# Six more small slots ahead of the stage pools, and a later place in the queue for the first seven-product pair's loads

## The chip, the cores and the metric

The kernel runs on one core of one Trainium2 chip. The metric is the device time of one execution in microseconds (us), the median of several runs. A profile records one further execution with the start and duration of every instruction and every DMA packet; it shows five engines: TensorE (PE for its matmuls, PEld for the loads of their stationary operands), VectorE (DVE), ScalarE (ACT), GpSimd (POOL) and SyncE (SP, which here only issues DMAs).

## What is computed

A decoder layer over 256 tokens of width 2048, batch 1, all in float32: a half-step SwiGLU block, a mixer (dilated attention beside gated linear attention, with one input and one output projection), cross-attention into 256 memory tokens, and a second half-step SwiGLU block.

```python
def swiglu(h, w_gate, w_up, w_down):
    return (jax.nn.silu(h @ w_gate) * (h @ w_up)) @ w_down

for l in range(DEPTH):                       # DEPTH = 1
    x = x + 0.5 * swiglu(rms_norm(x, ffn1_norm[l]), ffn1_w_gate[l], ffn1_w_up[l], ffn1_w_down[l])
    x = x + hybrid_mixer(rms_norm(x, mix_norm[l]), ...)
    x = x + cross_attention(rms_norm(x, xattn_norm[l]), rms_norm(mem, mem_norm[l]), ...)
    x = x + 0.5 * swiglu(rms_norm(x, ffn2_norm[l]), ffn2_w_gate[l], ffn2_w_up[l], ffn2_w_down[l])
return x
```

The gate and up weights of each SwiGLU block are 2048 x 5632, the down weights 5632 x 2048; together they are most of the 392 MB that the kernel reads.

## The kernel before

**Precision.** Every float32 operand of the large products is split in two parts, a high part rounded to the matmul's fp32r type and the low rest (`hi`, `lo`; `wh`, `wl` for weights). A product is three matmuls: high by high, high by low, low by high. In each, the moving operand is a 128 x 512 piece of a weight (`wh` or `wl`) and the stationary operand a 128 x 128 block of activations. ACT makes `wh` by a copy that rounds, DVE makes `wl` by a subtraction, both in halves of 128 x 1024 of a weight tile `raw` of 1 MiB that a DMA brought.

**Stages.** A SwiGLU block runs over eleven chunks `f` of 512 hidden columns. For `f == 0` `proj` (lines 165 to 181) makes gate and up in turn from four weight tiles each, loaded by `wgroup` (line 142). For every other `f`, `seven` (lines 249 to 286) makes gate and up together as a 2 x 2 block product with seven block products in place of eight (`product`, lines 223 to 227) and four plain ones (`plain`); its weight tiles are called `b11`, `b21`, `b12` and `b22` in the code, and DVE adds tiles to `b11` in place (`add`, line 205). After each of three segments of chunks, `proj` with the down weights runs over the chunks' hidden values `hT`. "The first pair" below is the gate and up of chunk `f == 1` in the first block, the first call of `seven`.

**What sets the order.** The kernel is written as one program, and a planner orders it for each engine by priority: an instruction's place in the program, less an offset that `tc.high_priority(n)` gives. Weight loads and splits of `wgroup` and the splits of `parts` have offset `WPRI = 200`; the loads of `seven`, through `load` (line 187), have `LPRI = 400`; the loads of `x` have `XPRI = 170` less 12 a chunk. All loads but one kind go through SP's queue in that order; the exception is the gate tile that POOL's queue adds to `b12` in memory (line 209). A load also needs a free buffer. The 1 MiB tiles have four buffers (`RB = 4`) that `wgroup` and `load` share; three tiles of each `seven` (`b11`, `b12`, `b22`, marked `True`) have three buffers of their own in a stage pool (`RX = 3`).

**Where tiles lie.** Pools are laid out along a partition in the order in which they are opened: `con` (constants, the residual `x`, and the transposed input `xTh`/`xTl`), `wp` (`raw`, `wh`, `wl`), `sp` (small work tiles of 2 KiB), `st` (statistics of 4 to 16 bytes, ten slots), and then the pools of a stage, opened by `enter` (lines 69 to 76): `u`, 26 or 32 slots of 2 KiB, and in the two SwiGLU blocks `r`, the three 8 KiB buffers above. The layout of the compiled kernel before, in bytes within a partition:

| tiles | pool | first address | past a multiple of 512 |
|---|---|---|---|
| `xTh`, `xTl` (stationary) | `con` | 33,824 | 32 |
| `raw`; `wh`; `wl` (moving) | `wp` | 67,104; 99,872; 116,256 | 32 |
| ten slots of 32 bytes | `st` | 149,024 | 32 |
| `hTh`, `hTl`, `Fh`, `Fl`, `mTh`, `mTl`, `memh`, `meml`, `oh`, `ol` (stationary) and others | `u` | 149,344 | 352 |
| `b11`, `b12`, `b22` | `r` | 202,592 | 352 |

All slots of these pools are a multiple of 512 bytes long, and each 128 x 128 block takes 512 bytes of a partition, so every block of a pool starts at the same distance past a multiple of 512. `hT` are the hidden values (stationary operand of the down projection), `F` three of the five differences of activation blocks that `seven` uses (the other two are written over blocks of `xTh`/`xTl` in `con`, line 388), `mT` the mixer's heads (output projection), `mem` the memory tokens, `o` the cross-attention's heads.

Of the kernel before, what the change touches and what calls it, by code (L numbers as in the profile page):

```python
# [27 lines left out]
WPRI = 200  # L28
LPRI = 400
# [25 lines left out]
def layer_kernel(ctx: ExitStack, tc: tile.TileContext, A: dict, out: bass.AP):  # L55
# [3 lines left out]
    con = ctx.enter_context(tc.tile_pool(name="con", bufs=1))  # L59
    wp = ctx.enter_context(tc.tile_pool(name="wp", bufs=3))  # L60
    sp = ctx.enter_context(tc.tile_pool(name="sp", bufs=SB))
    st = ctx.enter_context(tc.tile_pool(name="st", bufs=10))
    pa = ctx.enter_context(tc.tile_pool(name="pa", bufs=4, space=PSUM))
    pm = ctx.enter_context(tc.tile_pool(name="pm", bufs=4, space=PSUM))

# [12 lines left out]
    def U(shape, dt, name):  # L78
        return stage["u"].tile(shape, dt, tag="u", name=name)

    def raw_tile(long=False):

        if long and "r" in stage:
            return stage["r"].tile([P, 4, 512], F32, tag="rawx", name="raw")
        return wp.tile([P, 4, 512], F32, tag="raw", name="raw", bufs=RB)
# [3 lines left out]
    def W2(shape, name, dt=F32):  # L89
        return sp.tile(shape, dt, tag="w", name=name)  # L90
# [4 lines left out]
    def PM(shape, name):  # L95
        return pm.tile(shape, F32, tag="ps", name=name)
# [4 lines left out]
    def later(n, fn):  # L101
        pend.append([n, fn])
# [81 lines left out]


    def load(src, long=False):
        with tc.high_priority(LPRI):
            raw = raw_tile(long)
            SY.dma_start(raw, src)
        return raw  # L190
# [12 lines left out]
    def add(dst, src):  # L203
        with tc.high_priority(WPRI):
            V.tensor_add(dst, dst, src)  # L205

    def add_hbm(dst, src):
        with tc.high_priority(WPRI):
            G.dma_start(dst, src, accum_op=ALU.add)

    def urgent(op, *args, **kw):

        with tc.high_priority(FPRI):
            op(*args, **kw)  # L214
# [8 lines left out]
    def product(bank, form, raw, start):  # L223

        for h, half in enumerate(parts(raw)):
            mms(bank, form, half, start and h == 0, h == 1)
            tick()

    def plain(banks, forms, raw, start, order):
        for h, half in enumerate(parts(raw)):  # L230
            for t in order:
                mms(banks[t], forms[t], half, start[t] and h == 0, h == 1)
            tick()
# [4 lines left out]
    def difference(x, name, home=None):  # L238

        a, b = PAIRS[name]  # L240
        with tc.high_priority(WPRI):
            d = W2([P, 4, P], "d")
            V.tensor_sub(d, x[a], x[b])
            hi, lo = home or (U([P, 4, P], F32R, "Fh"), U([P, 4, P], F32R, "Fl"))
            SC.copy(hi, d)
            V.tensor_sub(lo, d, hi.bitcast(F32))
        return hi, lo

    def seven(ld, F, A12, A21, pair, others, rest):

        k1, k2 = pair
        Y, Z, X, R = [pa.tile([P, 512], F32, tag="acc", name="acc") for _ in range(4)]
        b11 = load(ld(0, k1), True)
        b21 = load(ld(0, k2))
        add(b11, b21)
        product(Y, A21, b11, True)
        s21 = W2([P, 512], "s21")
        urgent(SC.copy, s21, Y)  # L260
        b12 = load(ld(1, k1), True)
        product(Z, F["22-21"], b21, True)
        add(b11, b12)
        product(Y, F["12-21"], b11, False)
        s22 = W2([P, 512], "s22")
        urgent(SC.copy, s22, Y)
        b22 = load(ld(1, k2), True)
        product(X, F["22-12"], b22, True)
        add(b11, b22)
        product(R, A12, b11, True)  # L270
        urgent(V.tensor_sub, s22, R, s22)
        product(Y, F["21-11"], b12, False)
        add_hbm(b12, ld(0, k1))
        s12 = W2([P, 512], "s12")
        urgent(SC.copy, s12, Y)
        for k in others:
            plain((R, X), (rest(0, k), rest(1, k)), load(ld(1, k)), (False, False), (1, 0))
        urgent(V.tensor_sub, s12, R, s12)
        urgent(V.tensor_add, s22, X, s22)
        for k in others[:-1]:  # L280
            plain((Y, Z), (rest(0, k), rest(1, k)), load(ld(0, k)), (False, False), (1, 0))
        product(Y, F["11-12"], b12, False)
        k = others[-1]
        plain((Y, Z), (rest(0, k), rest(1, k)), load(ld(0, k)), (False, False), (0, 1))
        urgent(V.tensor_add, s21, Z, s21)
        return Y, s21, s12, s22

    def split_from_psum(hi, lo, ps):
        SC.copy(hi, ps)
        V.tensor_sub(lo, ps, hi.bitcast(F32))  # L290
# [70 lines left out]
    def ffn(pre, r, after, fine=None, last=False):  # L361
        wg, wu, wd = (A[f"{pre}_w_{n}"] for n in ("gate", "up", "down"))
        hT = {}
        F, xf = {}, {}

        def turn(f, hs):
            for t in range(TT):
                hi = U([P, 4, P], F32R, "hTh")
                lo = U([P, 4, P], F32R, "hTl")
                tp = PM([P, 4, P], "tp")  # L370
                for j in range(4):
                    PE.transpose(tp[:, j], hs[t][:, j * P:(j + 1) * P], ident)  # L372
                split_from_psum(hi, lo, tp)
                hT[f, t] = (hi, lo)

        def x_block(t, c):
            return tuple(p[:, :, t * P:(t + 1) * P] for p in xT[c])

        def x_differences(names):

            if not xf:
                for c in range(2):
                    for t in range(TT):
                        xf[t, c] = U([P, 4, P], F32, "xf")
                        hi, lo = (p.bitcast(F32) for p in x_block(t, c))
                        with tc.high_priority(WPRI):
                            V.tensor_add(xf[t, c], hi, lo)
            homes = {"21-11": x_block(1, 1), "11-12": x_block(0, 0)}
            for name in names:
                F[name] = difference(xf, name, homes.get(name))  # L390

        def lhs_h(k, t):
            return tuple(p[:, k % 4] for p in hT[k // 4, t])

        for seg in SEGS:
            for f in seg:
                if f == 0:
                    acc = proj(wg, f, lhs_x, range(4), fine)
                    if callable(r):
                        r = r()  # L400
                    later(DIFF, lambda: x_differences(("22-21", "12-21", "22-12")))
                    later(DIFF + 4, lambda: x_differences(("21-11", "11-12")))
                else:
                    y, s21, s12, s22 = seven(lambda col, k: (wg, wu)[col][f, k], F, x_block(0, 1), x_block(1, 0),
                                             (0, 1), (2, 3), x_block)
                    acc = [y, s21]
                sg = []
                for t in range(TT):
                    s = acc[t] if f and t else W2([P, 512], "sg")
                    urgent(SC.activation, s, acc[t], AF.Silu, scale=r[:, t:t + 1])  # L410
                    sg.append(s)
                acc = [s12, s22] if f else proj(wu, f, lhs_x, range(4))
                hs = []
                for t in range(TT):
                    h = acc[t] if f else W2([P, 512], "h")
                    urgent(V.scalar_tensor_tensor, h, acc[t], r[:, t:t + 1], sg[t], op0=ALU.mult, op1=ALU.mult)
                    hs.append(h)
                later(TURN, lambda f=f, hs=hs: turn(f, hs))
            final = seg is SEGS[-1]
            for c in range(NC):  # L420
                acc = proj(wd, c, lhs_h, seg, last=last and final and c == NC - 1)
                for t in range(TT):
                    V.scalar_tensor_tensor(xs[c][:, t], acc[t], 0.5, xs[c][:, t], op0=ALU.mult, op1=ALU.add)
                if final:
                    after(c)
# [57 lines left out]

    ss2 = new_ss("ss2")
    ffn("ffn1", load_x, lambda c: norm_chunk(c, xs[c], 16, ss2), fine=first)
    r2 = rstd_of(ss2, "r2")
    enter(u=UM)
# [479 lines left out]
    def store(c):  # L967
        for t in range(TT):
            SC.dma_start(out[0, t * P:(t + 1) * P, c * 512:(c + 1) * 512], xs[c][:, t])

    ffn("ffn2", r4, store, last=True)
    stage["stack"].close()
    assert not pend
# [83 lines left out]
```

## Time and profile before

| | |
|---|---|
| median of 3 runs | 1977.75 us (1976.2 to 1978.92) |
| the profiled execution's own time | 1978.33 us |
| its span, first to last instruction | 1976.2 us |
| granted TensorE clock, mean | 0.997 of full speed |
| DVE busy | 1377.3 us (70%) |
| ACT busy | 1062.0 us (54%) |
| POOL busy | 78.9 us (4%) |
| moved by DMA | 395.24 MB, 200 GB/s on average |

The views used below: the page with the busy time of each engine and the chain of work that ended last; the timeline, one row for an instruction or a run of equal ones, with its start and duration in us, engine, line, operation, tiles and, in brackets, the idle time before it and what ended that; the stretches, with the busy time of each engine and in brackets its instructions, then the granted clock, the DMA engines' share and their rate; and the groups of instructions by line with their count, busy time and mean duration. A matmul's recorded duration is longer than the distance from its start to the next one's start, since matmuls overlap; that distance is called the pitch here.

### The profile page before, as it was taken

Reading aid. Unit: us, or ns where it says so; the run is one execution under the profiler, and the core shown is the slowest. Engines: PE = TensorE matmul, PEld = TensorE weight load, DVE = VectorE, ACT = ScalarE, POOL = GpSimd, SP = SyncE. Lnnn points to the kernel's source line nnn. Section 1 sums busy time; section 2 is a strip of 40 time slices with the busy share of each in tenths; the row PEclk is TensorE's granted clock in tenths of the full one; section 3 lists DMA queues with packets and bytes.
Section 4 is the critical chain, followed back from the end, with each engine's and each line's share of the span. In section 5 each row is a group of like instructions: output and inputs, shape, how many; then the busy total and the mean of one; then the engine's idle time right before and its main releaser. Section 6 shows DMA issues by size and latency. Waiting matters only on the chain.

```text
span 1976.2 us, 22472 instructions
## 1 busy us (share of the span) xinstructions
PE 1951.9 (99%) x8760; PEld 1582.7 (80%) x8760; DVE 1377.3 (70%) x1423; ACT 1062.0 (54%) x1305; POOL 78.9 (4%) x81
## 2 busy tenths in 40 slices
PE   8999999999999999999999999999999999999999
PEld 6788887888878888778888779888887888887787
DVE  5888568885588664546785465888747888568863
ACT  5566346654356546544575365656634655436642
POOL 1000000000000000002220000000000000000000
PEclk9999999999999999999999999999999999999999
DMA  9566546775556554435465454666654766546563
GB/s 362 171 229 239 180 160 224 224 247 199 192 192 213 174 181 171 171 134 202 174 230 194 181 181 150 234 212 214 234 190 162 223 234 234 193 169 213 192 211 108
DMA packets 60566, 395.24 MB, mean 200 GB/s; under 512 B 6795, under 2 KB 7947, under 8 KB 14252
## 3 DMA queue, kind: packets, MB, share of 16 engines
q1 hardware_dynamic: 56428, 370.74, 51.4%
q0 software_dynamic: 2880, 20.97, 5.8%
q10 hardware_dynamic: 1152, 2.10, 0.3%
q8 instruction: 68, 1.11, 0.2%
q14 instruction: 38, 0.31, 0.0%
HBM read 391.69 MB, written 2.10 MB: 199 GB/s over the span
## 4 chain that ended last, share of the span: by engine, by line
PE 81%; DVE 12%; issue 3%; DMA 2%; ACT 2%; POOL 0%; SPq 0%; ACTq 0%; POOLq 0%
PE acc L161 17%; PE acc L163 17%; PE acc L162 17%; PE acc L220 9%; PE acc L221 9%; PE acc L219 9%; DVE wl L200 7%; DVE raw L205 2%; DMA raw<-in_ffn_w_gate_dram 2%; DVE s L214 1%; ACT wh L199 1%; DVE hTl L290 1%; PE tp L330 0%; DVE wl L153 0%; PE tp L372 0%
## 5 line engine op out<-in xcount | busy, mean ns | idle before, releaser
L153 DVE TENSOR_TENSOR wl<-raw,wh 128x1024 fp32r<-128x1024 f32 (+1 forms) x370 | 452.5, 1226 | 377.0 <-ACT wh L152 375.0
L152 ACT CAST wh<-raw 128x1024 fp32r<-128x1024 f32 (+1 forms) x370 | 386.5, 1047 | 466.8 <-PE acc L163 403.6
L199 ACT CAST wh<-raw 128x1024 fp32r<-128x1024 f32 x440 | 456.4, 1053 | 307.2 <-PE acc L221 251.3
L200 DVE TENSOR_TENSOR wl<-raw,wh 128x1024 fp32r<-128x1024 f32 x440 | 522.1, 1220 | 87.9 <-ACT wh L199 84.2
L220 PE MATMUL acc<-wl,xTh 128*128 128x512 f32 x960 | 375.8, 391 | 5.0 <-DVE wl L200 4.1
L219 PE MATMUL acc<-wh,xTh 128*128 128x512 f32 x960 | 375.9, 392 | 0.7
L221 PE MATMUL acc<-wh,xTl 128*128 128x512 f32 x960 | 373.7, 389 | 0.0
L161 PE MATMUL acc<-wh,hTh 128*128 128x512 f32 x704 | 278.3, 395 | 0.0
L163 PE MATMUL acc<-wh,hTl 128*128 128x512 f32 x704 | 277.5, 394 | 0.0
L162 PE MATMUL acc<-wl,hTh 128*128 128x512 f32 x704 | 277.5, 394 | 0.0
L161 PE MATMUL acc<-wh,xTh 128*128 128x512 f32 x544 | 217.0, 399 | 8.4 <-ACT wh L152 6.1
L220 PEld LDWEIGHTS acc<-wl,xTh 128*128 128x128 f32 x960 | 180.2, 188 | 50.0 <-DVE wl L200 13.0
L219 PEld LDWEIGHTS acc<-wh,xTh 128*128 128x128 f32 x960 | 180.2, 188 | 45.8 <-ACT wh L199 8.9
L163 PE MATMUL acc<-wh,xTl 128*128 128x512 f32 x544 | 214.3, 394 | 0.9 <-DVE xTl L314 0.9
L162 PE MATMUL acc<-wl,xTh 128*128 128x512 f32 x544 | 214.6, 394 | 0.3 <-DVE wl L153 0.3
L221 PEld LDWEIGHTS acc<-wh,xTl 128*128 128x128 f32 x960 | 180.2, 188 | 37.0
L205 DVE TENSOR_TENSOR raw<-raw 128x2048 f32<-128x2048 f32 x60 | 137.3, 2289 | 55.3 <-DMA raw<-in_ffn_w_gate_dram 54.6
L163 PEld LDWEIGHTS acc<-wh,hTl 128*128 128x128 f32 x704 | 131.7, 187 | 32.6
L162 PEld LDWEIGHTS acc<-wl,hTh 128*128 128x128 f32 x704 | 131.8, 187 | 32.2
L161 PEld LDWEIGHTS acc<-wh,hTh 128*128 128x128 f32 x704 | 131.7, 187 | 32.0
L161 PEld LDWEIGHTS acc<-wh,xTh 128*128 128x128 f32 x544 | 103.5, 190 | 30.9 <-ACT wh L152 6.1
L163 PEld LDWEIGHTS acc<-wh,xTl 128*128 128x128 f32 x544 | 103.4, 190 | 23.0 <-DVE xTl L314 1.3
(279 smaller groups left out, 1793.4 us busy)
## 6 DMA issues: line engine op xcount, KB each, us to landing
raw<-in_ffn_w_up_dram SPq DMA_DIRECT2D x88, 1024.0 KB, 4.9
raw<-in_ffn_w_down_dram SPq DMA_DIRECT2D x88, 1024.0 KB, 4.8
raw<-in_ffn_w_gate_dram SPq DMA_DIRECT2D x85, 1024.0 KB, 4.8
raw<-in_w_in_dram SPq DMA_DIRECT2D x48, 1024.0 KB, 4.8
raw<-in_ffn_w_gate_dram POOLq DMA_DIRECT2D x20, 1024.0 KB, 8.9
raw<-in_w_out_dram SPq DMA_DIRECT2D x16, 1024.0 KB, 4.8
raw<-in_xattn_w_k_dram SPq DMA_DIRECT2D x4, 1024.0 KB, 4.8
raw<-in_xattn_w_q_dram SPq DMA_DIRECT2D x4, 1024.0 KB, 4.8
```

Source lines behind the costliest of these rows:

```text
L152: SC.copy(wh[:, d], src)
L153: V.tensor_sub(wl[:, d], src, wh[:, d].bitcast(F32))
L161: PE.matmul(acc[t], lh, wh, start=first and i == 0, stop=False)
L162: PE.matmul(acc[t], lh, wl, start=False, stop=False)
L163: PE.matmul(acc[t], ll, wh, start=False, stop=last and i == len(half) - 1)
L199: SC.copy(wh, src)
L200: V.tensor_sub(wl, src, wh.bitcast(F32))
L205: V.tensor_add(dst, dst, src)
L214: op(*args, **kw)
L219: PE.matmul(bank, hi[:, k], wh, start=start and i == 0, stop=False, skip_group_check=True)
L220: PE.matmul(bank, hi[:, k], wl, start=False, stop=False, skip_group_check=True)
L221: PE.matmul(bank, lo[:, k], wh, start=False, stop=stop and i == len(half) - 1, skip_group_check=True)
```

## The change

The pool `st` gets 16 slots in place of 10, and the offset with which `load` places its loads becomes a variable. It is `WPRI` for chunk 1 of the first block and `LPRI` for all others, as before.

```diff
-    st = ctx.enter_context(tc.tile_pool(name="st", bufs=10))
+    st = ctx.enter_context(tc.tile_pool(name="st", bufs=16))
...
     def load(src, long=False):
-        with tc.high_priority(LPRI):
+        with tc.high_priority(ahead[0]):
             raw = raw_tile(long)
             SY.dma_start(raw, src)
         return raw
...
+    ahead = [LPRI]
...
                 else:
+                    ahead[0] = WPRI if f == 1 and pre == "ffn1" else LPRI
                     y, s21, s12, s22 = seven(lambda col, k: (wg, wu)[col][f, k], F, x_block(0, 1), x_block(1, 0),
                                              (0, 1), (2, 3), x_block)
```

With slots of 32 bytes, six more of them put the first address of `u` at 149,536 and that of `r` 192 bytes higher too, 32 bytes past a multiple of 512. No instruction is added or taken away, and the pools opened before `st` stay where they are.

## The prediction

> **What bounds the kernel now.** I read the page first: how busy each engine is, and which engine the chain of work that ended last runs through.
>
> ```profile
> span 1976.2 us, 22472 instructions
> PE 1951.9 (99%) x8760; PEld 1582.7 (80%) x8760; DVE 1377.3 (70%) x1423; ACT 1062.0 (54%) x1305; POOL 78.9 (4%) x81
> PE 81%; DVE 12%; issue 3%; DMA 2%; ACT 2%; POOL 0%; SPq 0%; ACTq 0%; POOLq 0%
> ```
>
> PE is busy for all but 24 us, and four fifths of the chain are its own. So time goes only if matmuls follow each other faster, or if one of the few places goes where PE waits. The change offers one of each.
>
> To see how fast matmuls follow each other I took two long stretches without a wait from the timeline, one with stationary operands in pool `u` (`hT`), one with stationary operands in `con` (`xT`), and asked the view of the stretches for their counts.
>
> ```profile
> 202.74 0.40 PE L162 MATMUL acc<-wl,hTh 128*128 128x512 f32 x1
> 286.04 0.39 PE L162 MATMUL acc<-wl,hTh 128*128 128x512 f32 x1
> 1258.47 0.39 PE L163 MATMUL acc<-wh,xTl 128*128 128x512 f32 x1
> 1299.07 0.39 PE L220 MATMUL acc<-wl,xTh 128*128 128x512 f32 x1
> ```
>
> ```profile
> 202.75:286.20 83.45, 83.45 (x359) 66.91 (x358) 45.17 (x40) 31.61 (x32) 0.00 (x0) 1.00 0.51 177
> 1258.50:1299.20 40.70, 40.70 (x181) 33.70 (x180) 33.08 (x38) 23.57 (x28) 0.70 (x1) 1.00 0.56 203
> ```
>
> A matmul's record lasts longer than the pitch, so a count also holds the matmul before the stretch's first row, which is still running. From the row at 202.74 to that at 286.04 there are therefore 359 - 2 = 357 pitches: 83.30 / 357 = 0.2333 us. From 1258.47 to 1299.07 there are 181 - 2 = 179: 40.60 / 179 = 0.2268. The clock is 1.00 in both, PE never waits, shapes and moving operands (`wh`, `wl`) are the same. A matmul whose stationary block lies in `u` costs **6.5 ns more**. By the layout the two kinds differ in the distance past a multiple of 512 (352 against 32) and in the region of the partition (above 149 KB against 34 to 67 KB). The trace cannot part these two, and that is the main uncertainty.
>
> The second place is at the start.
>
> ```profile
> 10.48 0.33 SPq L189 DMA_DIRECT2D raw<-in_ffn_w_gate_dram  x1
> 12.53 1.02 SPq L189 DMA_DIRECT2D raw<-in_ffn_w_up_dram  x2
> 14.48 0.33 SPq L142 DMA_DIRECT2D raw<-in_ffn_w_gate_dram  x1
> 15.14 1.62 SPq L304 DMA_DIRECT2D xr<-in_xT_dram  x2
> ```
>
> ```profile
> 28.42 1.99 ACT L152 CAST wh<-raw 128x1024 fp32r<-128x1024 f32 x2 [7.82 <-DMA raw<-in_ffn_w_gate_dram]
> 29.42 3.02 POOL L312 TENSOR_TENSOR xr<-xr,gain 128x512 f32<-128x512 f32 x2 [10.43 <-DMA xr<-in_xT_dram]
> 28.50 0.39 PE L163 MATMUL acc<-wh,xTl 128*128 128x512 f32 x1
> 31.16 0.50 PE L161 MATMUL acc<-wh,xTh 128*128 128x512 f32 x1 [2.28 <-ACT xTh L313]
> 33.04 0.80 PE L163 MATMUL acc<-wh,xTl 128*128 128x512 f32 x1 [0.95 <-DVE xTl L314]
> 39.17 0.40 PE L162 MATMUL acc<-wl,xTh 128*128 128x512 f32 x1
> ```
>
> ```profile
> 28.50:39.20 10.70, 7.47 (x19) 5.24 (x18) 7.99 (x7) 7.33 (x11) 3.02 (x2) 0.68 1.03 407
> DMA packets 3419, 14.47 MB, mean 414 GB/s; under 512 B 323, under 2 KB 323, under 8 KB 2205
> ```
>
> The last line is the DMA view of 12 to 47 us: the engines are saturated at 414 GB/s. Three 1 MiB loads of the first pair (10.48, 12.53) stand ahead of the fourth gate tile of chunk 0 (14.48) and the last blocks of the input (15.14), which land near 28.4 and 29.4 and are what ACT and POOL wait for. PE stops after 28.50, restarts in pieces, and then runs at a lower granted clock: 0.68 over the stretch.
>
> **The change part by part.** *A, the shift.* It moves no pool but `u` and `r`. The products with a stationary block in `u`, one row of each kind of three equal ones:
>
> ```profile
> L161 PE MATMUL acc<-wh,hTh 128*128 128x512 f32 x704 | 278.3, 395 | 0.0
> L219 PE MATMUL acc<-wh,Fh 128*128 128x512 f32 x240 | 96.8, 403 | 1.2 <-ACT wh L199 1.2
> L161 PE MATMUL acc<-wh,mTh 128*128 128x512 f32 x128 | 51.0, 399 | 0.9 <-DVE x L885 0.9
> L161 PE MATMUL acc<-wh,memh 128*128 128x256 f32 x64 | 18.6, 290 | 0.0
> L161 PE MATMUL acc<-wh,oh 128*128 128x512 f32 x32 | 12.9, 404 | 0.0
> L161 PE MATMUL acc<-wh,memh 128*128 128x512 f32 x32 | 12.8, 401 | 0.0
> ```
>
> - `hT`: 3 x 704 = 2112 by 6.5 ns = 13.7 us. The group has no idle time: PE sets the pace, so it counts in full.
> - `mT`, `oh`, `memh` at 512 columns: 3 x (128 + 32 + 32) = 576 by 6.5 = 3.7 us; `memh` at 256 columns: 192 by half of it, an estimate, 0.6 us.
> - `F`: 720 by 6.5 = 4.7 us at most, and none of it if something else sets the pace there. I asked for the chain of one pair:
>
> ```profile
> 106.58 1.24 DVE wl L200
> 122.28 1.23 DVE wl L200
> 123.55 0.50 PE acc L220
> ```
>
> ```profile
> 113.81 0.48 PE L219 MATMUL acc<-wh,Fh 128*128 128x512 f32 x1
> 123.10 0.39 PE L221 MATMUL acc<-wh,Fl 128*128 128x512 f32 x1
> ```
>
> From 106.58 to 123.51 the chain is on DVE (`wl`, the additions to `b11`, the evacuations) and comes back to PE only at 123.55; all `F` matmuls of the pair run from 113.81 to 123.10, beside it. A quicker `F` matmul only waits longer for `wl`. I take **0 of the 4.7**.
>
> The new pitch in `u` is not shown. Bounds: 0.2333 (nothing gained) and 0.2268 (the row of `con`); a rise is the third rival below. I take 0.2268, as that row has the very offset, 32, that `u` will have. The other instructions on shifted tiles do not care, by the rows of the one subtraction that writes to both places:
>
> ```profile
> L246 DVE TENSOR_TENSOR Fl<-d,Fh x6: 685/686/693, 53.3 to 1281.5; 128x512 fp32r<-128x512 f32 x6
> L246 DVE TENSOR_TENSOR xTl<-d,xTh x4: 683/686/687, 56.2 to 1287.9; 128x512 fp32r<-128x512 f32 x4
> ```
>
> Behind a quicker `hT` stretch nothing is late: in its row above DVE is busy 45.17 and ACT 31.61 of 83.45 us, and DMA takes 0.51. Six more slots of `st` cost no instruction, and the change adds no wait. Sum of A: 13.7 + 3.7 + 0.6 = **18.0 us** (18.0 to 22.7 if it works).
>
> *B, the loads.* All loads of the first pair lose 200 places. Three of them move in SP's queue from ahead of the gate tile at 14.48 to behind everything of chunk 0: that gate tile, two input blocks and four up tiles (and the four loads of `x`); POOL gets its `xr` earlier too. Three tiles are 3.15 MB; at 414 GB/s that is 7.6 us. So the gate tile lands near 28.4 - 7.6 = 20.8 and the input blocks near 21.8; from the last landing to PE's third restart it took 33.04 - 29.42 = 3.6 us, so all is ready at 25.4, **3.1 us before** PE ends at 28.50. The stop goes, and the lower clock that followed it. From 28.50 to 39.17 PE began 17 matmuls after the first (19 in the stretch's row, less the one still running and the first itself); at 0.2268 these take 3.9 us in place of 10.67: **6.8 us** gained.
>
> What can be late next is the first pair itself. Its first work is an addition to `b11`:
>
> ```profile
> 59.18 2.29 DVE L205 TENSOR_TENSOR raw<-raw 128x2048 f32<-128x2048 f32 x1
> ```
>
> It would start 6.8 us earlier, at 52.4. Queued in the new order, up to and with the pair's four tiles: the input 2.1 MB, gate and up 8.4, `x` 2.1, the four 4.2, together 16.8 MB; at 414 GB/s 40.6 us, about 45 us with a slower start (an estimate). That is 7 us of cover; without it each late 1 MiB costs 2.5 us. Bounds of B: 0 (the stop comes back elsewhere) to 6.8.
>
> Sum: 18.0 + 6.8 = 24.8. The profiled execution took 1978.33 us (its span and 2.1 around it), so 1953.5; it lies 0.6 above the median of the runs, so **1952.9 us** for the median.
>
> **A rule against A.** The Trainium skill, "TensorE: Matmul & The Clock Gate", section "Step-by-step: what each phase is for", says that TensorE has two independent read ports and that loading the next stationary operand takes no bandwidth from the running matmul; "SBUF — State Buffer", section "Specifications (TRN2)", gives lines of 16 bytes, of which 352 and 32 both are multiples. By these the offset would change nothing and A would bring 0. This trace does not agree with so simple a picture: equal shapes at an equal clock stand at 0.2333 and 0.2268. What no row excludes is that the region, and not the offset, makes the difference.
>
> **The rivals.**
> 1. *A does nothing*, since the region decides: `u` stays above 149 KB and its pitch at 0.2333. For it: the two kinds differ in both ways. Against, this row of the tile view (minimum, median and maximum duration): `hT` tiles lie in slots all over `u`, and the 704 durations keep within 5 ns, as if the one thing that all slots share decided.
>
> ```profile
> L162 PE MATMUL acc<-wl,hTh x704: 393/394/398, 196.3 to 1971.4; 128*128 128x512 f32 x176
> ```
>
>    Time: 1977.75 - 6.8 = 1971.
> 2. *B is given back* in the first pair. Its later loads now have offset 200, while the second pair's first loads keep 400. A pair is some 250 places long (180 matmuls and some 70 others, by the code), so those rank about 250 - 200 = 50 places behind the first pair's first load, ahead of its plain tiles, and can take one of the four shared buffers. A plain tile then comes late, PE stops as it did after 28.50, and the price is the same 6.8 us. For it: the inversion of ranks. Against: plain tiles are used behind five of the seven products, and three shared buffers stay. Time: 1977.75 - 18.0 = 1959.7.
> 3. *Slower.* The moving operands lie at 32 too. If `u`'s blocks collide with them there, the pitch rises by another step of 6.5 ns: 2112 + 576 + 192 / 2 = 2784 pitches, 18.1 us, against B's 6.8. It decides as soon as the pitch goes above 0.2333 + 6.8 / 2784 = 0.2357. Against: `con` is at 32 with the same moving tiles and has the shorter pitch. Time: 1977.75 - 6.8 + 18.1 = 1989.
> 4. *Neither part does what it says*: region decides and the stop moves: 1978.
> 5. *`F` counts as well*: 4.7 us more, 1948.
>
> **How the numbers follow.** Forecast 0.62, its own range 1949 to 1957. Rival 1 0.10, 2 0.13, 3 0.06, 4 0.04, 5 0.05. The forecast with rivals 2 and 5 makes 0.80; the range reaches from 1946 (rival 5 and 2 us) to 1962 (rival 2 and 2 us). Faster by over 0.2% (about what a measurement of this kernel can tell from no change): forecast, 1, 2 and 5, 0.90. Same: rival 4, 0.04. Slower: rival 3, 0.06.
>
> **What would show it.** A right: `hT` follows at 0.227, and 357 pitches of such a stretch take 81.0 us. A wrong: still 0.233. B right: the gate tile of line 142 is issued ahead of the loads of line 189, no wait of PE for `xTh L313` near 28 us, and no lower clock there. B given back: a new wait of PE in the first pair. If `F` counts, the pitch from one pair to the next shrinks by 0.24 us.

## The result, and the profile after

The changed kernel's median is **1955.26 us** (four runs, 1953.51 to 1955.79), against 1977.05 (four runs, 1976.2 to 1978.92) for the kernel before in the same comparison: a ratio of 0.9887, 95% interval 0.987 to 0.9904, or 21.8 us less by the medians. The forecast was 1952.9. The profiled execution took 1953.51 us; it is the fastest of the four, and the other three took 1.4 to 2.3 us more.

From the page of the changed kernel: span, busy time of the engines, and the engines' shares of the chain that ended last.

```profile
span 1951.6 us, 22473 instructions
PE 1927.6 (99%) x8760; PEld 1582.3 (81%) x8760; DVE 1377.3 (71%) x1423; ACT 1063.6 (54%) x1305; POOL 78.5 (4%) x81
PE 81%; DVE 12%; issue 3%; ACT 2%; DMA 1%; SPq 0%; POOL 0%; ACTq 0%; DVEq 0%; POOLq 0%
```

PE lost 24.3 us of busy time with the same 8760 matmuls, while DVE, ACT and POOL did as much as before. So matmuls follow each other faster; nothing was taken off another engine. (The instructions differ by one in number because the two kernels have a different number of semaphore waits.)

**The pitch.** Two stretches of equal length in the changed kernel: 205 to 275 us, all matmuls on `hT`, and 28.5 to 39.2 us, where the kernel before had its stop. The columns are those of the prediction (length, then PE, PEld, DVE, ACT and POOL busy with their counts, clock, DMA share, GB/s). The kernel before follows for the first stretch.

```profile
205.00:275.00 70.00, 70.00 (x311) 57.95 (x310) 38.30 (x34) 27.44 (x26) 0.00 (x0) 1.00 0.52 189
28.50:39.20 10.70, 10.70 (x49) 8.87 (x48) 6.50 (x6) 7.62 (x17) 0.00 (x0) 1.00 1.03 419
```

```profile
205.00:275.00 70.00, 70.00 (x302) 56.10 (x301) 36.70 (x33) 26.25 (x25) 0.00 (x0) 1.00 0.54 187
```

311 matmuls in place of 302 fit into 70 us at the same clock of 1.00. Over the whole trace, at full clock, the mean distance between the starts of two uninterrupted 512-column matmuls was 233.32 ns before with a stationary block in `u` (3272 pairs) and 227.06 with one in `con` (4353); after, it is 227.02 for all 7663. In the second stretch PE is busy throughout, with a clock of 1.00 in place of 0.68.

**The loads.** Of the changed kernel's timeline: SP's queue, the two instructions that had waited for the late tiles, the first pair's first addition, and the first and the last `F` matmul of the pair that the prediction looked at. Columns: start and duration in us, engine, line, operation, tiles, count, and the idle time before.

```profile
9.62 0.42 SPq L142 DMA_DIRECT2D raw<-in_ffn_w_gate_dram  x1
11.83 1.02 SPq L307 DMA_DIRECT2D xr<-in_xT_dram  x2
...
29.70 2.18 SPq L189 DMA_DIRECT2D raw<-in_ffn_w_gate_dram  x2
31.92 9.84 SPq L189 DMA_DIRECT2D raw<-in_ffn_w_up_dram  x4
51.78 0.33 SPq L189 DMA_DIRECT2D raw<-in_ffn_w_gate_dram  x1
...
20.32 1.05 ACT L152 CAST wh<-raw 128x1024 fp32r<-128x1024 f32 x1 [0.46 <-DMA raw<-in_ffn_w_gate_dram]
20.97 3.05 POOL L315 TENSOR_TENSOR xr<-xr,gain 128x512 f32<-128x512 f32 x2 [2.72 <-DMA xr<-in_xT_dram]
51.62 2.28 DVE L205 TENSOR_TENSOR raw<-raw 128x2048 f32<-128x2048 f32 x1
105.94 0.48 PE L219 MATMUL acc<-wh,Fh 128*128 128x512 f32 x1
115.24 0.39 PE L221 MATMUL acc<-wh,Fl 128*128 128x512 f32 x1
```

The gate tile and the input (lines 142 and 307, formerly 304) stand ahead of the pair's loads (line 189), and land about 8 us earlier, by the starts of the two instructions that wait for them (28.42 to 20.32, 29.42 to 20.97). The two first gate tiles and four up tiles of the first pair are queued from 29.70 on; the next tile on line 189, one of the pair's last two, only at 51.78. The addition starts 7.56 us earlier (59.18 to 51.62). The `F` matmuls take 9.30 us from first to last, where they took 9.29 before: nothing of their quicker pitch arrives in this pair.

**Where the 24.6 us of this profile were gained** shows in the tile view, by the first and last start of each kind (the two numbers behind "x704: 387/389/395," are the microseconds of the first and the last). First the kernel before, then the changed one; the row of `hTh` before stands in the prediction.

```profile
L161 PE MATMUL acc<-wh,mTh x128: 393/398/482, 1075.7 to 1171.9; 128*128 128x512 f32 x128
L161 PE MATMUL acc<-wh,memh x96: 276/281/481, 1049.1 to 1225.1; 128*128 128x256 f32 x64, 128*128 128x512 f32 x32
L161 PE MATMUL acc<-wh,oh x32: 388/398/587, 1225.4 to 1250.6; 128*128 128x512 f32 x32
```

```profile
L162 PE MATMUL acc<-wl,hTh x704: 387/389/395, 188.4 to 1946.8; 128*128 128x512 f32 x176
L161 PE MATMUL acc<-wh,mTh x128: 389/389/481, 1060.1 to 1154.3; 128*128 128x512 f32 x128
L161 PE MATMUL acc<-wh,memh x96: 278/283/481, 1034.0 to 1208.2; 128*128 128x256 f32 x64, 128*128 128x512 f32 x32
L161 PE MATMUL acc<-wh,oh x32: 389/389/580, 1208.5 to 1233.1; 128*128 128x512 f32 x32
```

The lead is the start in the kernel before less the start of the same matmul in the changed one. Before the first down projection it is 196.3 - 188.4 = 7.9 us; at the first `mem` product 1049.1 - 1034.0 = 15.1; at the last `mT` product 17.6; at the last 256-column `mem` product only 1225.1 - 1208.2 = 16.9; at the last `o` product 17.5; at the last `hT` product 24.6. So the start brought 7.9, the stretch of the first block's down projections 7.2, `mT` and the 512-column `mem` products 2.5, `o` 0.6, and the stretch of the second block's down projections 7.1; the 256-column `mem` products cost 0.7.

### The profile page after: what moved, and what is told of

The parts are those of the page before. It is cut to its first block, busy times and chain, and to the rows that moved or that the text cites. A ratio compares the mean times of both kernels' runs of the same rounds, so it can differ in the third digit from the quotient of the medians.

```text
span 1951.6 us, 22473 instructions
## 1 busy us (share of the span) xinstructions
PE 1927.6 (99%) x8760; PEld 1582.3 (81%) x8760; DVE 1377.3 (71%) x1423; ACT 1063.6 (54%) x1305; POOL 78.5 (4%) x81
## 3 DMA queue, kind: packets, MB, share of 16 engines
q0 software_dynamic: 2880, 20.97, 5.7%
## 4 chain that ended last, share of the span: by engine, by line
PE 81%; DVE 12%; issue 3%; ACT 2%; DMA 1%; SPq 0%; POOL 0%; ACTq 0%; DVEq 0%; POOLq 0%
PE acc L161 17%; PE acc L163 17%; PE acc L162 17%; PE acc L220 9%; PE acc L221 9%; PE acc L219 9%; DVE wl L200 7%; DVE raw L205 3%; DVE s L214 1%; ACT wh L199 1%; DVE hTl L293 1%; PE tp L333 1%; DMA raw<-in_ffn_w_gate_dram 0%; DVE wl L153 0%; PE tp L375 0%
## 5 line engine op out<-in xcount | busy, mean ns | idle before, releaser
L220 PEld LDWEIGHTS acc<-wl,xTh 128*128 128x128 f32 x960 | 180.2, 188 | 49.7 <-DVE wl L200 12.9
L221 PEld LDWEIGHTS acc<-wh,xTl 128*128 128x128 f32 x960 | 180.2, 188 | 36.9
L162 PEld LDWEIGHTS acc<-wl,xTh 128*128 128x128 f32 x544 | 102.7, 189 | 21.8 <-DVE wl L153 1.4
```

The costliest lines, as they stand in the source:

```text
L162: PE.matmul(acc[t], lh, wl, start=False, stop=False)
L220: PE.matmul(bank, hi[:, k], wl, start=False, stop=False, skip_group_check=True)
L221: PE.matmul(bank, lo[:, k], wh, start=False, stop=stop and i == len(half) - 1, skip_group_check=True)
```

## The experiments

What was open: the two parts had not been seen apart, and what it is about the shift that counts. The region of the pool fell with the result, as `u` is still above 149 KB. Three theories were left: that the offset of the stationary block itself decides (the first); that the distance between moving and stationary operand does (the second); that a moving tile costs more when it begins in the middle of a line of 64 bytes (the third). Each experiment is told as a diff against the changed kernel; three dots stand for lines left out. For the pitches, every matmul of a trace was put beside the addresses of its two operands in the compiled kernel; a mean is over uninterrupted 512-column matmuls.

### Each part alone

The shift alone (e1), then the loads alone (e2):

```diff
-        with tc.high_priority(ahead[0]):
+        with tc.high_priority(LPRI):
...
```

```diff
-    st = ctx.enter_context(tc.tile_pool(name="st", bufs=16))
+    st = ctx.enter_context(tc.tile_pool(name="st", bufs=10))
```

> Only the 16 slots of st; all loads keep offset 400. Theory (the two parts are independent): the pitch of hT, mT, mem, o and F is 0.2268 as in the changed kernel, the stop after 28.5 us stays, and the gain is that of the pitch alone, about 17 us: 1960 us. Rival (the shift also works through where tiles of the first stage lie, or needs the later loads): under 14 us or over 20 us.

> Only the later place of the first pair's loads; st keeps ten slots. Theory: hT stays at 0.2333, the stop at 28.5 us is gone, and the kernel gains what the changed kernel had gained by the first 100 us, 7.8 us: 1969 us. Rival (the loads' gain is partly given back further on): under 6 us, with a new wait before the first down projection at about 190 us.

The shift alone: 1960.46 us against 1977.27, ratio 0.9916 (0.9901 to 0.9931), **16.8 us less**. The loads alone: 1971.26, ratio 0.9968 (0.9956 to 0.9981), **6.0 us less**, where 7.8 had been expected; the interval reaches from 3.8 to 8.7 us. The two stretches, of the shift alone and then of the loads alone:

```profile
28.50:39.20 10.70, 7.86 (x26) 5.75 (x25) 8.45 (x7) 7.25 (x11) 3.02 (x2) 0.84 1.02 405
205.00:275.00 70.00, 70.00 (x311) 57.97 (x310) 37.41 (x33) 26.94 (x26) 0.00 (x0) 1.00 0.53 190
```

```profile
28.50:39.20 10.70, 10.70 (x49) 8.85 (x48) 6.44 (x7) 7.79 (x16) 0.00 (x0) 1.00 1.03 417
205.00:275.00 70.00, 70.00 (x302) 56.10 (x301) 36.33 (x33) 26.18 (x25) 0.00 (x0) 1.00 0.53 186
```

The shift has 311 matmuls on `hT` but keeps the stop, the loads have no stop but 302. The stop was shorter in this profile of the shift alone than in that of the kernel before (26 matmuls at a clock of 0.84 in place of 19 at 0.68), although the edit does not touch it: in this execution the low clock ended sooner. Together the parts bring 22.8, against 21.8 measured for both: they add up within the scatter.

### One operand at many offsets

Slots of `u` 2,080 bytes long, so that its blocks lie at 32, 64 and so on (s1), then slots of `wh` and `wl` 4,160 bytes long (m1):

```diff
-                        xf[t, c] = U([P, 4, P], F32, "xf")
+                        xf[t, c] = U([P, 520], F32, "xf")[:, 0:512].rearrange("p (a b) -> p a b", b=P)
...
```

```diff
+    def WT(m, n, name):
+        w = wp.tile([P, 1040], F32R, tag=name, name=name, bufs=WB)
+        return w[:, 0:1024].rearrange("p (m n) -> p m n", n=n)
...
-                wh = wp.tile([P, m, n], F32R, tag="wh", name="wh", bufs=WB)
...
+                wh = WT(m, n, "wh")
...
```

> The changed kernel with slots of u 2,080 bytes long in place of 2,048, so that the 26 slots begin at 32, 64, 96 and so on past a multiple of 512, while the moving tiles stay at 32. One run shows the pitch for every offset of the stationary block. Theory 1 (the block's own offset decides, by whether its 512 bytes cross a border unevenly): low at 0 and 32, 0.2333 or more at the offsets far from a multiple of 512. Theory 2 (the distance to the moving operand's offset decides): low at 32 alone, rising with the distance to both sides. The region as the cause fell already: in the changed kernel u is where it was, but for 192 bytes, and follows at 0.2268.

> The changed kernel with slots of wh and wl 4,160 bytes long in place of 4,096: the eight moving tiles begin at 32, 96, 160 up to 480 past a multiple of 512; all stationary blocks stay at 32. Theory 1 (the stationary block's own offset decides): the pitch stays at 0.2268 for all eight. Theory 2 (the distance decides): 0.2268 for the tile at 32, 0.2333 for the one at 224 (the distance of the kernel before with its sign turned), others between.

With the stationary blocks spread over the sixteen multiples of 32, one run took 1968.59 us. Over pairs of matmuls whose blocks lay at the same offset, the pitch was 227.0 ns at 32, and 230.3 to 234.8 at the other fifteen, 0 and 64 among them. This doesn't decide: the high and the low part of a product lay at different offsets, so that neighbours mix. With the moving operand spread and all stationary blocks at 32, one run took 1983.54 us, longer than the kernel before. The mean pitch by the moving operand's offset:

```
offset   32     96     160    224    288    352    416    480
ns      229.2  229.9  232.1  233.3  229.5  229.3  233.3  233.3
```

The theory of the stationary block's own offset falls: nothing about it changed here, and the pitch moved by up to 4 ns. These means too hold matmuls whose neighbour lay at another offset, so they say that the moving operand matters, but not how. One thing in them stays unexplained: 32 and 288 lie 0 and 256 bytes from the stationary blocks, and yet stand at 229, not 227. Here `wh` and `wl`, which take turns as the moving operand, lie 256 bytes apart from each other; in the layouts that follow they do not.

### The two operands against each other

The next four put every operand at one offset at a time. `st` with 15 slots puts `u` at 0, with 8 at 288; a wider `gain` tile in `con` puts all pools 480 bytes further, at 0; and the last moves `wp` alone to 0 and leaves every stationary block at 32. The diffs of e3 (e4 has 8 in place of 15), e5 and e6:

```diff
-    st = ctx.enter_context(tc.tile_pool(name="st", bufs=16))
+    st = ctx.enter_context(tc.tile_pool(name="st", bufs=15))
```

```diff
-    gain = con.tile([P, 82], F32, name="gain")
+    gain = con.tile([P, 202], F32, name="gain")[:, 0:82]
```

```diff
-    st = ctx.enter_context(tc.tile_pool(name="st", bufs=16))
+    st = ctx.enter_context(tc.tile_pool(name="st", bufs=17))
...
-        r = con.tile([P, TT], F32, name=name)
+        r = con.tile([P, 122 if name == "r4" else TT], F32, name=name)[:, 0:TT]
```

> The changed kernel with 15 slots of st: u and r begin at a multiple of 512, the moving tiles and con stay at 32. Theory 1 (the block's own offset decides, by the borders that its 512 bytes cross): 0.2268 or less for hT, as it crosses none. Theory 2 (the distance to the moving operand decides): the distance is 32 in place of 0, so hT rises, to 0.230 or more.

> The changed kernel with 8 slots of st: u and r begin at 288, a distance of 256 to the moving tiles. Theory 1: 0.2333 for hT, as at 352. Theory 2, if the distance repeats at 256: 0.2268; if it does not: 0.230 or more.

> The changed kernel with 480 unused bytes behind the gains, the first tile of con: xT, the moving tiles, u and r all begin at a multiple of 512. Theory 2 (the distance decides, 0 as in the changed kernel): 0.2268 for xT and hT, the time of the changed kernel, 1955 to 1957. Theory 1: the blocks cross no border any more, 0.2268 or less. Theory 3 (a moving tile in the middle of a line of 64 bytes costs as well): under 0.222 everywhere, and a time under 1930.

> The moving tiles at a multiple of 512, all stationary blocks (xT and u) at 32, by 480 unused bytes behind con and 17 slots of st. Theory 2: the distance is 32, xT and hT both rise above 0.2268, to 0.230 or more, and the kernel is slower than the changed one by 7800 matmuls by 3 to 6 ns, 25 to 50 us. Theory 1: 0.2268, and the changed kernel's time. Theory 3: below 0.2268.

The stretch of `hT` from 205 to 275 us, in the order e3, e4, e5, e6 (one fence for each kernel):

```profile
205.00:275.00 70.00, 70.00 (x301) 56.23 (x301) 36.35 (x33) 26.23 (x25) 0.00 (x0) 1.00 0.53 186
```

```profile
205.00:275.00 70.00, 70.00 (x310) 57.96 (x309) 37.96 (x34) 26.71 (x27) 0.00 (x0) 1.00 0.53 194
```

```profile
205.00:275.00 70.00, 70.00 (x310) 57.98 (x309) 38.30 (x34) 27.30 (x26) 0.00 (x0) 1.00 0.53 193
```

```profile
205.00:275.00 70.00, 70.00 (x301) 56.35 (x301) 36.33 (x32) 26.33 (x26) 0.00 (x0) 1.00 0.50 180
```

In the table, a kernel whose stationary blocks all lie at one offset has one mean pitch, in ns, for both pools; "before" is the median of the kernel before in the same comparison.

| kernel | moving at | `con` at | `u` at | pitch `con` | pitch `u` | time, us | before, us |
|---|---|---|---|---|---|---|---|
| before | 32 | 32 | 352 | 227.06 | 233.32 | | 1977.05 |
| changed | 32 | 32 | 32 | 227.02 | 227.02 | 1955.26 | 1977.05 |
| e3 | 32 | 32 | 0 | 227.03 | 233.28 | 1973.25 (one run) | 1978.17 |
| e4 | 32 | 32 | 288 | 227.0 | 227.10 | 1955.2 (one run) | 1978.17 |
| e5 | 0 | 0 | 0 | 227.03 | 227.03 | 1955.36 | 1978.17 |
| e6 | 0 | 32 | 32 | 233.26 | 233.26 | 1998.88 | 1978.17 |

e5 has a ratio of 0.9887 (0.9872 to 0.9901), e6 one of **1.011** (1.0093 to 1.0127): 20.7 us slower than before. The own offset is out: a stationary block at 0 is slow in e3 and fast in e5, one at 32 is fast in the changed kernel and slow in e6. A 64-byte line is out as well, since 32 is as good as 0 when both operands have it. What is left is the distance between the two, 0 or 256 bytes in the fast rows. In each of these layouts a matmul's own stationary block and the next matmul's block lie at the same distance from its moving operand, and the next block is loaded beside the running matmul (in the kernel before, a matmul starts at 12.07 us and the next one's load at 12.08); so the runs do not say which of the two blocks counts.

### The distance, scanned

`u` at 288, `con` at 32, and a view that moves on in the slots of `wh` and `wl` every 24 halves:

```diff
+SHIFTS = (0, 4, 8, 12, 16, 24, 32, 40, 48, 52, 56, 60, 64)
...
-    st = ctx.enter_context(tc.tile_pool(name="st", bufs=16))
+    st = ctx.enter_context(tc.tile_pool(name="st", bufs=8))
...
+        w = wp.tile([P, 1088], F32R, tag=name, name=name, bufs=WB)
+        e = SHIFTS[made[0] // 2 // 24 % len(SHIFTS)]
+        made[0] += 1
+        return w[:, e:e + 1024].rearrange("p (m n) -> p m n", n=n)
...
```

> The changed kernel with u at 288, slots of wh and wl 4,352 bytes long (so that they begin at 32 or 288) and, within them, the tile begun 0, 16, 32, 48, 64, 96, 128, 160, 192, 208, 224, 240 or 256 bytes further on, another distance every 24 halves of a weight tile. All stationary blocks are at 32 or 288. Theory 2 with a period of 256 (e3 to e6): 0.2268 at 0 and 256 and 0.2333 at 32, 64, 192 and 224. If only a distance of 0 helps, all others, 128 too, stand at 0.2333; if the period is 128 or less, 128 stands at 0.2268. Theory 1 (own offset) gave the wrong answer in e5 and e6 and would give 0.2268 everywhere.

One run took 1988.71 us, against 1977.24 for the kernel before. The mean pitch by the distance (moving less stationary, modulo 256 bytes), with the count of matmuls that had a neighbour of the same distance on both sides:

```
bytes      0      16     32     48     64     96     128    160    192    208    224    240
ns       227.16 231.62 233.30 233.31 228.95 233.41 232.64 234.14 233.30 234.62 233.29 229.49
count     1119   631    711    820    706    643    590    624    456    430    428    455
```

Only a distance of 0 gives 227. Eight others give 232.6 to 234.6; 16, 64 and 240 lie between, and at 64 the expected 233.3 was missed by 4 ns. So the pitch does not only tell equal from unequal, and what orders the values between is not shown. The kernel before had 32 - 352 = -320, that is 192: 233.30 here, 233.32 there. e3 has 32 and e6 224: 233.30 and 233.29 here.

### What still stands in the first pair

After the change PE still runs at a lower clock once: 62 to 69 us (70 to 77 before), at the first pair. The stretch of the changed kernel, and its waits:

```profile
62.00:69.00 7.00, 4.84 (x13) 3.32 (x12) 7.00 (x8) 3.89 (x4) 0.00 (x0) 0.76 0.30 125
```

```profile
60.30 2.28 DVE L205 TENSOR_TENSOR raw<-raw 128x2048 f32<-128x2048 f32 x1
62.51 1.28 DVE L293 TENSOR_TENSOR hTl<-tp,hTh 128x512 fp32r<-128x512 f32 x2
62.68 3.89 ACT L199 CAST wh<-raw 128x1024 fp32r<-128x1024 f32 x4 [1.63 <-DVE raw L205]
63.77 0.50 PE L219 MATMUL acc<-wh,Fh 128*128 128x512 f32 x1 [1.40 <-ACT wh L199]
65.03 0.50 PE L220 MATMUL acc<-wl,Fh 128*128 128x512 f32 x1 [0.76 <-DVE wl L200]
```

DVE has no idle moment there, and the second addition to `b11` (60.30) holds up ACT's split (62.68), for which PE waits (63.77). Three tries to relieve it: the first addition on POOL (e8), that and the second addition ahead of the product in front of it (e9), and the earlier second addition with both on DVE (e10).

The first of these fences is in e8 and e9, the second in e9 and e10, where the new lines stand ahead of the product `Z`.

```diff
-        add(b11, b21)
+        if ahead[0] == WPRI:
+            with tc.high_priority(WPRI):
+                G.tensor_tensor(b11, b11, b21, op=ALU.add)
+        else:
+            add(b11, b21)
```

```diff
+        if ahead[0] == WPRI:
+            add(b11, b12)
...
-        add(b11, b12)
+        if ahead[0] != WPRI:
+            add(b11, b12)
```

> The changed kernel with the first addition of the first pair (b11 += b21, 2.28 us on DVE at 51.6 us) on POOL. Theory on what is left of part B: PE's stop of about 3 us at 62 us and the lower clock behind it come from DVE's chain in the first pair, so 2.3 us less on DVE bring 2.3 us or, with the clock, up to 5: 1950 to 1953. Rival (the stop is set by the landing of b12, or POOL's slower addition is late): no gain, 1955, or a loss of 2 us.

> e8 with the second addition of the first pair (b11 += b12) ahead of the splits of b21 on DVE. Theory: DVE's chain to the third product is shorter by the two splits of b21, 2.3 us, so that PE hardly stops and its clock stays: 5 to 6 us below the changed kernel, 1949 to 1951. Rival: the stop moves to the second product, which now waits for its own splits: as e8 or slower.

> The changed kernel with the second addition of the first pair (b11 += b12) ahead of the splits of b21, both additions on DVE as before. e8 and e9 showed that POOL's addition at 44 us takes 4.6 to 5.1 us and that a subtraction of DVE beside it takes 5.1 us in place of 0.7, which ate what DVE had been spared. Theory: without that, the shorter chain to the third product shortens PE's stop at 62 us from 3 us to 1 or 2 and leaves the clock up: 2 to 5 us below the changed kernel, 1951 to 1953. Rival: the stop only moves to the second product, and the clock falls there: 1955, as the changed kernel.

| kernel | us | range | ratio (95%) |
|---|---|---|---|
| changed | 1955.26 | 1953.51 to 1955.79 | 0.9887 (0.987 to 0.9904) |
| e8 | 1956.51 | 1955.43 to 1957.32 | 0.9895 (0.988 to 0.991) |
| e9 | 1954.31 | 1954.15 to 1954.98 | 0.9884 (0.9867 to 0.99) |
| e10 | 1954.64 | 1953.28 to 1955.36 | 0.9884 (0.9867 to 0.99) |

None can be told from the changed kernel, and none reached the 2 to 6 us that had been expected of it. In e8 the timeline shows what the move to POOL costs:

```profile
44.07 4.64 POOL L262 TENSOR_TENSOR raw<-raw 128x2048 f32<-128x2048 f32 x1 [0.47 <-DMA raw<-in_ffn_w_gate_dram]
44.15 5.12 DVE L243 TENSOR_TENSOR d<-xf 128x512 f32<-128x512 f32 x1
```

```profile
43.49 0.68 DVE L243 TENSOR_TENSOR d<-xf 128x512 f32<-128x512 f32 x1
```

DVE's subtraction, 0.68 us in the changed kernel (second fence), lasts 5.12 us while POOL adds: what DVE is spared it loses by waiting. This agrees with the Trainium skill, "SBUF — State Buffer", section "Who interferes with whom": a DVE operation and a POOL operation that need the port pair which they share don't divide it, the later one waits to the end of the earlier. Here the addition ends at 48.71 us and the subtraction at 49.27. In e10 the stretch that was 0.76 keeps its clock, but PE's wait comes a little later; the next two fences have two stretches of e10 and the rows of its waits.

```profile
62.00:69.00 7.00, 5.93 (x25) 4.59 (x26) 7.00 (x7) 4.86 (x6) 0.00 (x0) 1.00 0.41 150
70.00:77.00 7.00, 5.01 (x22) 3.69 (x21) 6.44 (x8) 6.00 (x7) 0.60 (x1) 1.00 0.71 241
```

```profile
62.99 0.50 PE L219 MATMUL acc<-wh,Fh 128*128 128x512 f32 x1 [1.42 <-ACT wh L199]
...
71.47 0.49 PE L219 MATMUL acc<-wh,xTh 128*128 128x512 f32 x1 [1.23 <-ACT wh L199]
72.72 0.50 PE L220 MATMUL acc<-wl,xTh 128*128 128x512 f32 x1 [0.76 <-DVE wl L200]
```

The clock stays up, and PE waits later instead. That the clock stays up can't be put down to the edit: it also did in e4, whose first pair is that of the changed kernel. The loads alone, without any of the three tries either, had 0.81 in the second stretch. The rows of e4, and then of the loads alone:

```profile
62.00:69.00 7.00, 4.84 (x20) 3.45 (x19) 7.00 (x7) 4.35 (x5) 0.00 (x0) 1.00 0.40 150
70.00:77.00 7.00, 5.02 (x21) 3.61 (x20) 5.83 (x5) 4.87 (x5) 0.00 (x0) 1.00 0.51 164
```

```profile
70.00:77.00 7.00, 5.12 (x16) 3.54 (x16) 5.83 (x5) 4.68 (x5) 0.00 (x0) 0.81 0.53 170
```

By its busy time in e10, 7.00 of 7.00 us from 62 us on and 6.44 from 70 us on, DVE remains the bound of this pair; shifting its work within the pair did not shorten it.

## Why the prediction was right

- **What bounds the kernel**: right. Both gains came from PE's own pace and from one stop of PE; the other engines' busy time is unchanged.
- **A, 18.0 us**: measured 16.8 alone (medians), and 24.6 - 7.9 = 16.7 by the profile. By the starts above, the stretches of the down projections brought 7.2 + 7.1 = 14.3, 13.8 of it between the first and the last `hT` matmul of each of the six (forecast 13.7), and `mT`, `oh` and `memh` at 512 columns 2.5 + 0.6 = 3.1 (3.7). The step that failed is "`memh` at 256 columns by half of it, an estimate, 0.6 us": it cost 0.7, since the lead fell from 17.6 to 16.9 there and the mean pitch of its 183 uninterrupted pairs rose from 116.8 to 120.6 ns. The sign was wrong, not only the size. The shorter pitch had been seen at 512 columns only, and halving it for 256 had no row behind it. The pitch fell by 6.3 ns in the mean, 6.5 in the two stretches of the prediction.
- **A's open question** was rival 1, that the region decides. It fell with the result: `u` stays above 149 KB and follows at 227.02. But the reason given for the forecast, that `u` will have "the very offset, 32" of `con`, was right for another cause than it sounds: 32 is nothing special (e5, e6), it is the moving operand's offset too. Rival 3 feared exactly that coincidence, and e6 shows that its opposite is true: apart is slow. Had the change put `u` at 0, its gain would have been B and little else (e3).
- **The rule against A**, which the prediction quoted from the Trainium skill, "TensorE: Matmul & The Clock Gate", section "Step-by-step: what each phase is for" (two read ports, no bandwidth taken from the running matmul), would have let the place of the operands change nothing. These runs don't agree: with the same matmuls, e6 and the changed kernel differ by 43.6 us by the place of the operands alone. Whether a load takes reads from the running matmul, no run shows. The line of 16 bytes that the Trainium skill gives in "SBUF — State Buffer", section "Specifications (TRN2)", doesn't explain it either, as all distances in the scan are multiples of 16.
- **`F`, 0 of 4.7**: right, by the two rows that span 9.29 and 9.30 us; over all pairs the stretches between the down projections added at most half a microsecond. Rival 5 is out. The `F` matmuls, paced by DVE's `wl`, gained next to nothing from their own speed.
- **B, 6.8 us**: right in mechanism. The tiles landed at 20.3 and 21.0 (forecast 20.8 and 21.8), and the addition came at 51.62 (52.4). Between the matmuls that the kernel before began at 28.50 and at 39.17, the lead grows by 6.8 us in the changed kernel and in the loads alone. But this price was read from one execution. In the shift alone, which keeps the stop, the same stretch was 1.8 us shorter than in the kernel before, mostly since the low clock ended sooner; against that execution the stop would be worth 5.0. Behind the stop, the first pair's waits move the lead again: in the loads alone it falls from 6.6 us at the 150th matmul to 5.3 at the 300th, in the changed kernel it goes from 7.5 to 7.9. The loads alone had a clock of 0.81 there, where e4, with much the same waits, has 1.00 (the rows of both are above). The profiled run of the loads alone is also the slowest of its six (1970.46 to 1973.07). So a microsecond or two of B hangs on when and how long the low clock falls; the prediction had no term for that.
- **Rival 2**, B given back by loads of the second pair that overtake: out. In the order of the compiled kernel all eight loads of the first pair stand ahead of the second pair's first, as they did before, so nothing overtook, and no new wait of the size of 6.8 us came up. The cover of 7 us before the first addition held.

The sum by the medians, 16.8 + 6.0 = 22.8, lies 2.0 below the forecast 24.8: 1.2 from A and 0.8 from B. By the times alone neither can be told from nothing (13.6 to 19.6 us for the shift, 3.8 to 8.7 for the loads); for A the profile agrees, since the 256-column products alone make 1.3 us of difference, while B's 0.8 is within its scatter. Both parts together brought 21.8, 3.0 below the forecast, and the kernel before was 0.7 us faster in this comparison than the median that the forecast started from; that makes up the 2.4 us above 1952.9. What stays open is why the distance matters: no run shows the mechanism behind it.

## What to carry to other kernels

Where PE is the bound, look up where the moving and the stationary operand start within a partition: for the 512-column fp32r matmuls of this kernel a distance of a multiple of 256 bytes, the same for all neighbours, gave the shortest pitch, and a small pool between two large ones can shift it by accident. Multiply such a difference only by the matmuls that PE itself paces, and only for the shapes in which it was seen. Where DMA is saturated at the start, look for loads of the next stage that queue ahead of the last of this one: here three of them held up PE, and putting them behind cost nothing, as their first use was far enough away. And a price that holds a stretch of low clock should not be read from one execution alone.

## What the runs showed that was not expected

- The pitch of 128 x 512 matmuls depends on the distance between their operands' addresses: 227.0 ns at a multiple of 256 bytes, 232.6 to 234.6 at most other distances, 229 at 64. Over a kernel of 8760 matmuls the best and the worst layout of e5 and e6 are 43.5 us apart.
- At 256 columns it was the other way round: 120.6 ns at a distance of 0 in the changed kernel, 116.8 in the kernel before.
- A POOL addition of 128 x 2048 (4.64 us) held a DVE subtraction that takes 0.68 us in the changed kernel: it took 5.12.
